# A two-layer decoder step on one core: the 796 steps of its attention stage in another order

## The chip, the core and the metric

The kernel runs on one core of a Trainium2 chip. The core has a matrix engine (TensorE, PE in the profile, its weight loads PEld), VectorE (DVE), ScalarE (ACT), GpSimd (POOL) and SyncE (SP), each with its own instruction queue that it works off in order, and 16 DMA engines that every queue's transfers share. The metric is the time of one execution in device microseconds, and lower is better.

## The reference

One inference step of a small decoder for two groups of tokens with the same weights: a prompt of 512 tokens, and 8 samples of one token each at position 2048, with a cache of 128 keys and values per sample. Two layers; each is half a SwiGLU, a mixer, half a SwiGLU. Layer 0 mixes by causal pooling, layer 1 by sliding-window attention with a sink per head. The change lies in layer 1's attention alone:

```python
kv = _rmsnorm(x, kv_norm_g) @ w_kv                       # shared keys and values, 4 heads of 64
...
h = _rmsnorm(x, norm_g[l, 1])
q = _rope((h @ w_q[j]).reshape(B, T, N_KV_HEADS, GROUP, HEAD_DIM), pos)      # 16 heads of 64
out = _window_attention(q, kk, vv, wb, pos0, attn_sinks[j]) @ w_o[j]
...
def _sink_attention(q, k, v, mask, sinks):
    s = jnp.einsum('bnqkgd,bnskd->bnkgqs', q, k) * (HEAD_DIM ** -0.5)
    s = jnp.where(mask, s, -jnp.inf)
    m = jnp.maximum(jnp.max(s, axis=-1, keepdims=True), sink)
    p = jnp.exp(s - m)
    denom = jnp.sum(p, axis=-1, keepdims=True) + jnp.exp(sink - m)
    return jnp.einsum('bnkgqs,bnskd->bnqkgd', p / denom, v)
```

D_MODEL is 1024, the window 128, everything float32.

## The kernel before, in words

Each float32 operand of a large product is split into a high part (ACT) and a low part (DVE), and a product is three passes: high by high, low by high, high by low. All 520 tokens lie along the free side of the tiles, so a matmul of the projections streams 260 columns.

The attention stage (`with tc.tile_pool(name="at" ...)`, from L1940) comes after layer 1's first half SwiGLU and before its second. Its work is cut into 796 steps. A step is a letter and a number: the letter is a function, the number which piece of it. The string `PLAN` (L61) lists them, and the loop at the end of the stage (L2349) emits them in that order. Since each emitted instruction is kept in program order (`later`), **the order of PLAN is the order in each engine's queue**, for DMAs on SP and POOL too; nothing reorders them. An engine whose first instruction waits holds up all behind it.

The steps that matter here:

- `q0` to `q63` (PE, L885): the query projection, 8 tiles t of 8 steps, 6 matmuls each. `o0` to `o63` (PE, L885): the output projection. These are the dense products.
- `e` (ACT, L1966) copies a finished query tile from PSUM to SBUF (`qraw`). For the rotary embedding the rotated rows of two or four tiles are gathered into one tile `qG` by small DMAs, 16 rows each: `a` on SP and `g` on POOL (L1974). `r` (DVE, L1980 to L1983, four instructions) rotates `qG`; `J` on SP and `I` on POOL (L1988) send the rows back. The tiles are gathered in three sets: `GATHERS = ((0, 1), (2, 3), (4, 5, 6, 7))`.
- `z`, `y` (L1992, L1995) split a tile's prompt queries. `k` (POOL, L2000) copies its sample queries to `qz`, two small copies a tile, `qz` 0 for tiles 0 to 3 and `qz` 1 for 4 to 7.
- Prompt attention goes in 16 units (a tile t, a half h of the blocks): `S` scores (PE, L2025), `N` sinks (POOL, L2034), `X` mask and minimum (DVE, L2044), `E` exponentials (ACT, L2061), `R` inverse (DVE), `C`, `c`, `p` scaling (L2072 on DVE or POOL, L2070 on ACT), `T` transposes (PE, L2083), `t`, `u` their splits (ACT L2088, DVE L2093), `V` products with the values (PE, L2110), `v`, `j` copies out (L2119).
- Sample attention: `10` to `17` scores (PE, L2158) with `b` (DVE, L2163); `20` a transpose, `B0`, `x0`, `D0` its softmax, `30` back, `d0`; `40` to `47` values (PE, L2204) with `f`. Steps `1` and `4` are matmuls that stream only 8 columns.
- `w`, `W` split weights (ACT L452, DVE L456); `l0` to `l6` (SP, L625) load the chunks of 1 MB in two DMAs (`raw`); `L0` (SP, L2283) loads the 1 MB of cached values (`vc`).
- `h`, `H`, `s`, `G` split the attention's output for `o`; `O` adds to the residual stream.

Some buffers are few: PSUM holds two double banks (query tiles, scores, output tiles) and four single ones (transposes, value products, sample products), `sm` (scores) has 3 buffers, `raw` 3, `qG` 1.

Of the kernel before, what the change touches and what calls it, by code (L numbers as in the profile page):

```python
# [58 lines left out]


PLAN = """  # L61
q0 N0 q1 q2 q3 q4 q5 q6 w6 W6 q7 e0 w10 W10 U0 q8 q9 q10 q11 q12 q13 Z0 w7 q14 q15 N1 w5 q16 g0 q17 q18 q19 a0
e1 w8 W5 q20 q24 q25 W8 q26 q27 W7 q28 q29 w15 g1 a1 r0 I0 J0 z0 y0 q21 q22 q23 e2 q30 q31 e3 S0 F0 I1 w9 S1
X0 X3 X1 X2 J1 q32 q33 q34 g3 E0 E1 S2 S3 W9 w11 w13 W13 X4 z1 y1 q35 q36 a2 X7 E2 q37 q38 E3 w12 q39 a3 g2 E4
X5 R0 e4 c1 X6 r1 W12 S4 S5 X8 q40 N2 X11 c2 c0 p3 X9 q41 W11 E6 X10 T0 T1 N3 t0 E8 q42 E5 l0 J2 w16 E7 I2 E9
W15 E10 E11 R2 C10 R1 c9 q43 q44 q45 I3 C5 c6 q46 q47 e5 C4 S6 S7 J3 l1 a4 z2 p11 X12 X15 T2 w14 t1 q48 p7 y2
X14 X13 k0 T3 t3 u1 t2 z3 q49 q50 E12 E14 W14 u0 E15 N4 E13 S8 S9 X16 W16 X18 p8 T4 X19 k3 k1 R3 C15 p13 k2
w18 t4 q51 q52 a5 L0 p12 u4 X17 E16 q53 q54 q55 E18 E17 e6 T5 S10 C14 S11 w17 q56 q57 t5 u5 q58 q59 q60 N5 u3
q61 q62 i0 q63 w19 g6 g5 X20 E20 X23 E23 X22 W17 g4 Q0 E19 R4 p18 c16 T6 T7 X21 E21 y3 a6 E22 R5 C21 C22 S12
C17 e7 u2 T8 t6 S13 g7 u6 p20 V0 W18 t8 V1 v0 V4 V5 t7 X24 a7 N6 X25 X27 u8 v1 p23 v5 v4 E24 E27 T10 r2 J4 J5  # L70
p19 w23 S14 J6 12 13 b1 t10 V2 V3 u10 v2 W19 T9 t9 S15 X26 v3 u7 I6 T11 E26 V6 t11 u9 I4 E25 J7 R6 X28 h0 N9
V8 V9 N7 X29 v9 E28 u11 z4 10 11 b0 I7 V7 X30 c25 X31 V10 y4 v6 E29 E30 I5 z5 y5 E31 V11 R7 p24 T12 t12 u12 v7
k4 h1 l2 S18 S19 v8 v10 X36 p26 p27 X37 v11 X38 S16 H1 k7 k5 k6 14 p29 T13 X39 E36 t13 16 17 b3 15 z7 p28 E38
S17 E37 b2 20 N8 p30 T14 u13 X32 V12 V13 S20 S21 p31 T15 B0 E39 R9 p37 p39 X33 x0 X35 X34 D0 30 t14 E32 u14
E35 S22 S23 y7 E33 d0 z6 p36 p38 y6 X40 X41 E34 40 42 N10 t15 u15 T18 R8 p34 p32 v13 X43 v12 E40 E43 E41 p33
T19 X44 X45 N11 43 41 f0 t19 X42 E42 u19 R10 44 45 h2 47 46 f1 s1 X47 t18 V14 S24 T16 c40 u18 t16 p35 T17 s2
c41 S25 X46 H2 H0 V18 G2 N12 X48 t17 X50 X49 p42 X51 E44 E45 V15 v14 S26 V19 s0 v15 u16 h3 H3 s3 G3 T20 G0 p43
E46 E47 G1 R11 E48 E51 S27 p44 T21 u17 p46 o0 o1 o2 E50 t20 X52 X55 c45 o3 O0 u20 V16 V17 X54 t21 p47 E49 v18
R12 v19 j16 j17 h4 l3 o4 T22 u21 p50 p48 p49 o5 s4 T23 X53 N13 o6 o7 C51 O1 t22 u22 S28 S29 T24 S30 S31 t23
X56 N14 X58 u23 w22 t24 X59 E52 E55 E53 X57 T25 E54 t25 u25 E56 R13 p53 N15 V22 V23 X60 o8 o9 o10 o11 c54 W23  # L80
u24 j23 V24 X62 X61 E57 V20 V21 X63 w21 p52 T26 W22 o24 E58 o25 c55 O2 o12 E60 E62 w28 o26 H4 E63 E59 t26 G4
v22 o27 E61 R15 R14 T27 j21 V25 p61 t27 u27 O6 p59 w26 o13 o14 o15 c63 w20 v20 h5 p58 C62 W20 v24 W26 H5 o16
o17 o18 w30 p60 T30 W21 C57 T31 t31 o19 O3 t30 C56 u31 u26 o28 o29 T28 t28 u28 T29 o30 t29 w24 u29 V26 o31 O4
V27 u30 V30 o20 o21 o22 W28 W30 v26 l4 V28 V31 v27 v25 o23 h6 H6 V29 s5 G5 W24 O7 O5 o32 o33 w25 j30 W25 s6
o36 o37 j31 w27 W27 v29 v28 h7 G6 H7 s7 G7 o34 o35 o38 O8 o39 O9 P0 Y0 o40 o41 A0 M0 A1 M1 w31 o42 W31 l5 o43
O10 P1 Y1 w35 W35 o44 o45 A2 M2 P2 Y2 o46 o47 O11 w36 W36 o48 o49 o50 o51 w29 W29 O12 P3 Y3 A3 M3 A4 M4 P4 w33
Y4 o52 o53 o54 o55 O13 W33 w32 W32 o56 P5 Y5 o57 o58 o59 O14 A5 P6 M5 o60 o61 Y6 o62 l6 o63 O15 A6 M6 w34 W34
P7 Y7 A7 M7
"""

GATHERS = ((0, 1), (2, 3), (4, 5, 6, 7))
# [2515 lines left out]
```

## Time and profile before

| what | time |
|---|---|
| runs | 1536.85, 1537.49, 1537.56 us (median 1537.49) |
| profiled execution | 1536.74 us |
| its span, first to last instruction | 1535.0 us |
| attention stage, first `q` to last `o` matmul | 1039.6 to 1197.5 us of the span |
| mean granted TensorE clock | 0.993 |

The profile's times are microseconds from the span's start. In the views by windows, each row is a stretch of the span: its length, then the busy time of each engine with the number of instructions, the granted clock of TensorE (1.00 is full speed), the mean busy share of the 16 DMA engines and GB/s. In the timeline a row is one instruction, or several alike: start, time taken, engine, line, operation, output tile <- input tiles, shapes, count, and in brackets the time for which the engine had sat idle before it and what ended that.

### The profile page before, as it was taken

The numbers are of one execution on the slowest core, as the hardware profiler recorded it, in microseconds if no ns is written. First come the engines' busy times: TensorE is split into PE (matmuls) and PEld (weight loads), VectorE is DVE, ScalarE is ACT, GpSimd is POOL, SyncE is SP. The second block draws the span as 40 slices with busy tenths as digits, with TensorE's granted clock in tenths as the row PEclk, the third lists the DMA queues.
The fourth block names the chain that finished last, engine by engine and source line by source line (L and its number), as shares of the span: only waits on it lengthen the run. The fifth ranks groups of instructions, "written<-read, shape, count | busy, mean of one in ns | idle before, by whom it ended". The sixth has DMA issues, their size and how long they took to land. (4 is left out here: it accounts for less than half of the span.)

```text
span 1535.0 us, 34974 instructions
## 1 busy us (share of the span) xinstructions
PE 1511.8 (98%) x13350; PEld 1496.5 (97%) x13350; DVE 1380.3 (90%) x2794; ACT 993.9 (65%) x2024; POOL 304.4 (20%) x346
## 2 busy tenths in 40 slices
PE   9999999999999999999999999999999999999997
PEld 9999999999999999999999999999889999999997
DVE  6999999879999999888999999886778899999976
ACT  6765765657775765656765665665776666666655
POOL 1122222001122222101322222101541122222200
PEclk9999999999999999999999999999979999999999
DMA  9589999754599999745899899763412589999941
GB/s 237 122 194 207 186 199 200 183 161 123 123 202 195 191 201 197 170 134 129 193 192 207 186 200 207 164 179 88 101 29 56 131 182 197 193 199 197 207 119 57
DMA packets 418837, 254.64 MB, mean 166 GB/s; under 512 B 13134, under 2 KB 399174, under 8 KB 418628
## 3 DMA queue, kind: packets, MB, share of 16 engines
q1 hardware_dynamic: 339390, 187.30, 44.2%
q0 software_dynamic: 75520, 60.00, 28.3%
q10 hardware_dynamic: 3758, 5.09, 1.1%
q8 instruction: 105, 1.72, 0.5%
q14 instruction: 64, 0.52, 0.1%
HBM read 218.07 MB, written 6.11 MB: 146 GB/s over the span
## 5 line engine op out<-in xcount | busy, mean ns | idle before, releaser
L452 ACT ACTIVATE wh<-raw 128x512 fp32r<-128x512 f32 (+1 forms) x724 | 445.9, 625 | 188.3 <-PE ps L915 105.9
L456 DVE TENSOR_TENSOR wl<-raw,wh 128x512 fp32r<-128x512 f32 (+1 forms) x724 | 488.1, 685 | 32.5 <-ACT wh L452 31.0
L915 PE MATMUL ps<-th,wh 128*128 128x260 f32 x1216 | 334.7, 275 | 2.5 <-DVE sb L1221 2.4
L915 PE MATMUL ps<-tl,wh 128*128 128x260 f32 x1216 | 334.4, 275 | 0.0
L915 PE MATMUL ps<-th,wl 128*128 128x260 f32 x1216 | 334.4, 275 | 0.0
L915 PE MATMUL ps<-xh,wh 128*128 128x260 f32 x896 | 246.8, 275 | 0.8 <-ACT ps L1195 0.5
L915 PE MATMUL ps<-xl,wh 128*128 128x260 f32 x896 | 246.6, 275 | 0.0
L915 PE MATMUL ps<-xh,wl 128*128 128x260 f32 x896 | 246.4, 275 | 0.0
L915 PEld LDWEIGHTS ps<-th,wh 128*128 128x128 f32 x1216 | 231.0, 190 | 3.1 <-DVE sb L1221 2.8
L915 PEld LDWEIGHTS ps<-th,wl 128*128 128x128 f32 x1216 | 231.0, 190 | 0.0
L915 PEld LDWEIGHTS ps<-tl,wh 128*128 128x128 f32 x1216 | 231.0, 190 | 0.0
L629 POOL DMA_DIRECT2D S<-in_ffn_w_up_dram x76 | 99.7, 1318 | 453.7 <-DMA S<-in_ffn_w_up_dram 145.8
L915 PE MATMUL ps<-hh,wh 128*128 128x260 f32 x656 | 181.1, 276 | 1.0 <-ACT ps L1260 0.7
L915 PE MATMUL ps<-hl,wh 128*128 128x260 f32 x656 | 181.1, 276 | 0.3 <-DVE hl L604 0.3
L915 PE MATMUL ps<-hh,wl 128*128 128x260 f32 x656 | 180.4, 275 | 0.0
L915 PEld LDWEIGHTS ps<-xh,wh 128*128 128x128 f32 x896 | 170.2, 190 | 1.4 <-ACT ps L1260 0.7
L915 PEld LDWEIGHTS ps<-xl,wh 128*128 128x128 f32 x896 | 170.2, 190 | 0.3 <-DVE xl L604 0.2
L915 PEld LDWEIGHTS ps<-xh,wl 128*128 128x128 f32 x896 | 170.2, 190 | 0.0
L352 POOL DMA_DIRECT2D raw<-raw x108 | 95.4, 883 | 337.2 <-DVE wl L456 89.0
L915 PEld LDWEIGHTS ps<-hh,wh 128*128 128x128 f32 x656 | 124.6, 190 | 2.2 <-ACT ps L1260 2.1
L915 PEld LDWEIGHTS ps<-hl,wh 128*128 128x128 f32 x656 | 124.6, 190 | 1.2 <-DVE hl L604 0.5
L915 PEld LDWEIGHTS ps<-hh,wl 128*128 128x128 f32 x656 | 124.6, 190 | 0.0
(380 smaller groups left out, 3669.0 us busy)
## 6 DMA issues: line engine op xcount, KB each, us to landing
raw<-in_ffn_w_gate_dram SPq DMA_DIRECT2D x87, 512.0 KB, 5.0
raw<-in_ffn_w_up_dram SPq DMA_DIRECT2D x87, 512.0 KB, 6.1
raw<-in_ffn_w_down_dram SPq DMA_DIRECT2D x128, 256.0 KB, 5.2
raw<-raw POOLq DMA_DIRECT2D x108, 256.0 KB, 4.5
S<-in_ffn_w_up_dram SPq DMA_DIRECT2D x76, 256.0 KB, 3.7
S<-in_ffn_w_up_dram POOLq DMA_DIRECT2D x76, 256.0 KB, 5.5
raw<-in_ffn_w_down_dram SPq DMA_DIRECT2D x16, 768.0 KB, 4.5
S<-in_ffn_w_down_dram SPq DMA_DIRECT2D x32, 256.0 KB, 4.0
```

The costliest lines, as they stand in the source:

```text
L352: G.dma_start(blk(raw, 2, 1), blk(raw, 1, 1), accum_op=ALU.add)
L452: self.pin(self.nc.scalar.activation(views[0], src, AF.Copy))
L456: self.pin(self.nc.vector.tensor_tensor(l, src, h.bitcast(F32), op=ALU.subtract))
L629: return [ld(lambda t: t, a), lambda t: nc.gpsimd.dma_start(t, b, accum_op=ALU.add)]
L915: T.matmul(bank[:, :H], a[:, kk, :], two(b), start=(not more and kk == 0 and i == 0), stop=(kk == 3 and i == 2), skip_group_check=more,)
```

## The change

`PLAN` alone is replaced. The 796 steps are the same, each once, with the same functions, engines, buffers and bytes; only their order is another. Two of the lines that are replaced, and two that replace them:

```diff
-k4 h1 l2 S18 S19 v8 v10 X36 p26 p27 X37 v11 X38 S16 H1 k7 k5 k6 14 p29 T13 X39 E36 t13 16 17 b3 15 z7 p28 E38
-S17 E37 b2 20 N8 p30 T14 u13 X32 V12 V13 S20 S21 p31 T15 B0 E39 R9 p37 p39 X33 x0 X35 X34 D0 30 t14 E32 u14
...
+R7 v10 S18 k5 z6 k6 p28 S19 X36 X39 X37 16 17 N8 E36 v9 E39 S17 X32 14 V6 X38 X33 p30 p29 b3 E38 X34 V7 X35
+p31 E37 v7 15 R9 v8 p39 p36 S20 b2 20 S22 h2 T14 p38 T15 B0 x0 t14 S23 D0 30 t15 S21 H2 d0 40 u14 v6 p37 V12
```

Three places show how it moves instructions.

**SP's queue of DMAs in the stage**, from the second set of gathers on (L1974 gathers, L1988 sends back, `raw` from `in_w_o_dram` is a weight chunk in two DMAs, `vc` the cached values). Before:

```order
L1974 DMA qG<-qraw 16x520 x2
L625 DMA raw_16128<-in_w_o_dram 64x4x512 x2
L1988 DMA qraw<-qG 16x520 x2
L625 DMA raw_16195<-in_w_o_dram 64x4x512 x2
L1974 DMA qG<-qraw 16x520 x2
L2283 DMA vc<-in_cache_v_win_dram 128x8x256
L1974 DMA qG<-qraw 16x520 x2
L1988 DMA qraw<-qG 16x520 x4
L625 DMA raw_16703<-in_w_o_dram 64x4x512 x2
```

Now:

```order
L625 DMA raw_15869<-in_w_o_dram 64x4x512 x2
L1974 DMA qG<-qraw 16x520 x2
L1988 DMA qraw<-qG 16x520 x2
L625 DMA raw_16269<-in_w_o_dram 64x4x512 x2
L2283 DMA vc<-in_cache_v_win_dram 128x8x256
L1974 DMA qG<-qraw 16x520 x4
L1988 DMA qraw<-qG 16x520 x4
L625 DMA raw_17209<-in_w_o_dram 64x4x512 x2
```

The first chunk (`l0`) now stands ahead of the second set's gathers, the second chunk and `vc` stand together ahead of all of the third set. The chunk behind the last four sends (`l2`) waited before for DVE's last split of an earlier chunk; it now takes the buffer of `vc`, and waits for the last sample value product (`46`).

**POOL's queue around the third set's sends** (L2072 is `p`, L2034 `N`, L2000 the copies to `qz`). Before:

```order
L1988 DMA qraw<-qG 16x520 x2
L2034 COPY sm<-nsinks 128x4 x2
L1988 DMA qraw<-qG 16x520 x2
L2072 TENSOR_SCALAR sm<-sm,den 128x128
L2000 COPY qz_15661<-qraw 64x8 x2
L2072 TENSOR_SCALAR sm<-sm,den 128x256 x2
L2000 COPY qz_15661<-qraw 64x8 x6
```

Now:

```order
L1988 DMA qraw<-qG 16x520 x3
L2034 COPY sm<-nsinks 128x4
L1988 DMA qraw<-qG 16x520
L2072 TENSOR_SCALAR sm<-sm,den 128x128
L2072 TENSOR_SCALAR sm<-sm,den 128x256 x2
L2034 COPY sm<-nsinks 128x4
L2000 COPY qz_15661<-qraw 64x8 x8
```

One `N` instead of two stands between the sends, and all eight copies to `qz` 1 stand together, behind three `p`.

**PE's queue at the sample values** (`40` to `47`, L2204, a row of x2 is one step). Before, with two pairs of transposes (L2083) between:

```order
L2204 MATMUL pv_16870<-prT,vc 128x8 x4
L2083 MATMUL pv_16880<-ident,sm 128x128 x4
L2083 MATMUL pv_16897<-ident,sm 128x128 x4
L2204 MATMUL pv_16870<-prT,vc 128x8 x4
L2204 MATMUL pv_16922<-prT,vc 128x8 x8
```

Now, from the first of them:

```order
L2204 MATMUL pv_16838<-prT,vc 128x8 x2
L2110 MATMUL pv_16844<-xh,tl 128x256 x2
L2110 MATMUL pv_16844<-xl,tl 128x256
L2204 MATMUL pv_16838<-prT,vc 128x8 x2
L2110 MATMUL pv_16844<-xh,tl 128x256 x2
L2110 MATMUL pv_16844<-xl,tl 128x256
```

Each step now has products with the values (L2110) or transposes beside it; six steps in a row have become at most two.

More of the change, by code (lines that the diff above doesn't have):

```diff
@@ L61 @@
 PLAN = """
[L62 to L71, printed above, removed]
@@ L72 @@
-V8 V9 N7 X29 v9 E28 u11 z4 10 11 b0 I7 V7 X30 c25 X31 V10 y4 v6 E29 E30 I5 z5 y5 E31 V11 R7 p24 T12 t12 u12 v7
-k4 h1 l2 S18 S19 v8 v10 X36 p26 p27 X37 v11 X38 S16 H1 k7 k5 k6 14 p29 T13 X39 E36 t13 16 17 b3 15 z7 p28 E38
-S17 E37 b2 20 N8 p30 T14 u13 X32 V12 V13 S20 S21 p31 T15 B0 E39 R9 p37 p39 X33 x0 X35 X34 D0 30 t14 E32 u14
-E35 S22 S23 y7 E33 d0 z6 p36 p38 y6 X40 X41 E34 40 42 N10 t15 u15 T18 R8 p34 p32 v13 X43 v12 E40 E43 E41 p33
-T19 X44 X45 N11 43 41 f0 t19 X42 E42 u19 R10 44 45 h2 47 46 f1 s1 X47 t18 V14 S24 T16 c40 u18 t16 p35 T17 s2
@@ L77 @@
[L77 to L86, printed above, removed]
@@ L87 @@
-Y4 o52 o53 o54 o55 O13 W33 w32 W32 o56 P5 Y5 o57 o58 o59 O14 A5 P6 M5 o60 o61 Y6 o62 l6 o63 O15 A6 M6 w34 W34
-P7 Y7 A7 M7
+N1 q8 N0 w5 q9 q0 q1 q2 q3 q4 q5 w13 q10 q11 q12 q6 q7 q13 q14 w6 W6 e0 g0 a0 w9 q15 e1 g1 U0 W5 q16 q17 a1 r0
+J0 I0 w10 W10 q18 q19 q20 Z0 J1 w7 W7 z0 y0 l0 I1 q21 q22 q23 e2 q24 q25 q26 q27 q28 q29 q30 q31 w8 S2 S3 F0
+e3 W8 X4 X7 X6 w15 N2 X5 q32 E4 q33 E6 W15 q34 q35 W9 E7 E5 R1 S0 S1 C5 z1 W13 X0 X2 C4 a3 X3 X1 c6 q36 q37 y1
+q38 g3 E0 E1 g2 T2 q39 E3 e4 a2 k0 S4 S5 t2 r1 w11 X8 w12 E2 R0 X9 c1 q40 q41 J2 c0 p7 c2 T3 t3 I2 q42 X11 W11
@@ new lines @@
+E8 E11 X10 E10 q43 q44 E9 I3 N3 T0 w14 u3 p3 S6 S7 W12 z2 X12 X15 X14 q45 J3 q46 q47 R2 z3 X13 y2 p8 E12 E13
+e5 E14 p11 W14 E15 R3 c9 C15 T1 t1 u2 q48 q49 q50 p12 k3 S8 T4 l1 q51 p13 C10 S9 w17 X16 C14 T5 t5 w16 L0 q52
+y3 t4 w22 q53 q54 q55 t0 N4 X18 E16 e6 a6 X19 E19 X17 E17 a4 k1 S10 g6 a5 u1 E18 S11 N5 k2 X20 X21 X23 E20 E23
+X22 g4 g5 R4 c16 Q0 C17 E22 W16 E21 W22 q56 q57 q58 q59 q60 q61 q62 p18 w18 q63 e7 u0 T6 u4 T7 t7 p19 S12 S13
+R5 V4 i0 g7 C22 t6 u5 V5 v5 10 N6 v4 u7 X24 a7 X26 p23 X25 11 E24 C21 X27 E27 E25 b0 r2 V2 V3 v3 p20 V0 v2 J4
@@ new lines @@
+u6 S14 I4 E26 T10 t10 T11 I6 I5 t11 u10 V1 v1 u11 N7 v0 S15 T8 w19 R6 T9 V10 I7 X28 X30 t8 u8 12 13 c25 V11 t9
+p24 E28 E30 X31 E31 V8 z4 J6 b1 u9 T12 t12 X29 p27 y4 V9 J5 p26 T13 t13 u13 S16 N9 v11 k4 J7 k7 z5 u12 E29 y5
+R7 v10 S18 k5 z6 k6 p28 S19 X36 X39 X37 16 17 N8 E36 v9 E39 S17 X32 14 V6 X38 X33 p30 p29 b3 E38 X34 V7 X35
+p31 E37 v7 15 R9 v8 p39 p36 S20 b2 20 S22 h2 T14 p38 T15 B0 x0 t14 S23 D0 30 t15 S21 H2 d0 40 u14 v6 p37 V12
+E32 41 E34 E33 u15 X40 X41 N10 V13 43 h0 E35 R8 p33 W17 X43 X42 E40 E41 v13 v12 V14 y6 T18 t18 E42 u18 V15 E43
@@ new lines @@
+p32 T16 S24 42 R10 v14 t16 T19 S25 p35 f0 v15 p34 u16 V16 p43 t19 h1 X44 X45 N11 E44 V18 T17 t17 u19 X46 E46
+X47 E47 44 47 h3 N12 X48 E45 c40 X51 X50 X49 V19 p42 u17 c41 v19 S26 S27 H1 v18 z7 45 46 R11 f1 s1 T20 T21 V17
+H0 s0 p47 G0 X52 s2 E48 G2 G1 H3 p44 o4 p46 t20 E50 X54 s3 G3 E51 c45 X55 X53 o5 E49 R12 o6 t21 o7 T22 u21 y7
+p50 o0 T23 t23 N13 E52 W19 C51 j16 O1 o1 E54 u20 o2 o3 E53 N14 O0 W18 E55 S28 S29 j17 o24 o25 o26 V20 o27 R13
+l2 X56 X59 X57 p49 p48 T24 X58 h4 c54 V21 S30 t22 u22 O6 E56 w23 W23 T25 t24 u24 t25 o8 o9 o10 o11 V22 j21 N15
@@ new lines @@
+p52 E57 E58 l3 u23 V23 S31 E59 R14 O2 p59 C56 w21 C57 T28 c55 u25 s4 o28 o29 o30 j23 X60 v20 w20 H4 X62 V24
+X61 v22 w24 p58 E60 X63 E63 T29 o31 W20 o16 t28 o17 t29 u29 p53 E61 E62 R15 c63 p61 W21 o18 h5 O7 H5 T26 u28
+T27 t27 u27 o19 C62 V25 w25 p60 T30 o12 T31 t30 u30 o13 o14 t26 s5 G5 o15 w31 W31 V30 t31 u31 V31 l4 O4 w29
+u26 V26 W24 V28 w26 W26 V27 v27 o20 o21 O3 o22 o23 G4 v25 o32 j30 V29 v24 v26 h6 o33 s6 W29 v29 G6 O5 W25 o36
+o37 v28 j31 h7 H6 o34 s7 H7 G7 o35 O8 w28 W28 w27 W27 o38 o39 o40 o41 o42 A0 M0 o43 P0 Y0 O9 O10 w30 W30 P1 Y1
@@ L89 @@
+A1 M1 P2 Y2 o48 o49 w32 o44 l5 l6 o45 o46 o47 o56 o57 W32 O11 w34 W34 A2 M2 o50 A3 M3 o51 O12 o52 P3 o53 Y3
+o54 o55 w36 W36 A4 M4 o58 P4 Y4 o59 O13 P5 w33 O14 Y5 o60 o61 W33 A5 M5 o62 w35 o63 O15 P6 Y6 A6 M6 A7 M7 P7
+Y7 W35
 """
```

## The prediction, made before the change was run

> **What bounds the kernel now.** I read the page first, for which engine is full. Its part on busy times, and in its slices the row of the granted clock:
>
> ```profile
> PE 1511.8 (98%) x13350; PEld 1496.5 (97%) x13350; DVE 1380.3 (90%) x2794; ACT 993.9 (65%) x2024; POOL 304.4 (20%) x346
> ...
> PEclk9999999999999999999999999999979999999999
> ```
>
> The matrix engine is full, so time can only come from its gaps, its clock or its work. The work is the same here. One slice, the 30th, has a clock of 0.7, and it lies in the attention stage. So I took the view by windows: the stage in three parts (query projection; attention proper; from the first `o` on), then short windows around the clock's edges.
>
> ```profile
> core 0: us, PE busy (x) PEld busy (x) DVE busy (x) ACT busy (x) POOL busy (x), PEclk, DMA share, GB/s
> 1039.60:1093.77 54.17, 53.37 (x492) 51.49 (x491) 37.66 (x109) 34.44 (x93) 16.06 (x35) 1.00 0.42 104
> 1093.77:1139.46 45.69, 41.95 (x317) 37.53 (x315) 33.89 (x116) 32.28 (x101) 23.39 (x40) 0.81 0.25 55
> 1139.46:1197.47 58.01, 57.95 (x521) 56.93 (x520) 47.79 (x106) 39.87 (x99) 10.82 (x16) 1.00 0.22 60
> 1113.12:1123.36 10.24, 9.56 (x50) 9.11 (x52) 8.09 (x31) 8.71 (x29) 6.99 (x9) 0.50 0.01 2
> 1130.19:1137.02 6.83, 6.83 (x35) 5.71 (x36) 5.43 (x22) 3.83 (x13) 2.33 (x3) 0.50 0.70 157
> ...
> 1126.77:1130.19 3.42, 3.42 (x33) 3.42 (x32) 3.06 (x16) 2.26 (x8) 3.11 (x5) 1.00 0.00 0
> 1109.71:1113.12 3.41, 0.58 (x12) 0.44 (x8) 0.54 (x1) 1.20 (x4) 0.74 (x4) 1.00 0.26 46
> ```
>
> All that is lost lies in the middle part: two stretches at clock 0.50, 10.24 and 6.83 us, though PE is "busy" in them. The last two rows are the 3.4 us ahead of each: before the first PE is almost idle, before the second it is busy throughout. PE's timeline says with what, and what half the clock does to a product:
>
> ```profile
> 1101.08 0.39 PE L2110 MATMUL pv<-xh,tl 128*128 128x256 f32 x2
> ...
> 1101.42 0.39 PE L2110 MATMUL pv<-xh,tl 128*128 128x256 f32 x2
> ...
> 1113.80 0.99 PE L2158 MATMUL pv<-qz,kc 128*128 128x8 f32 x4 [3.51 <-issue]
> ...
> 1120.73 0.63 PE L2110 MATMUL pv<-xh,tl 128*128 128x256 f32 x2
> ...
> 1121.37 0.63 PE L2110 MATMUL pv<-xh,tl 128*128 128x256 f32 x2
> ...
> 1127.01 2.74 PE L2204 MATMUL pv<-prT,vc 128*128 128x8 f32 x24
> ```
>
> Three value products start 0.34 us apart at full clock (1101.08 to 1101.42) and 0.64 us apart in the first stretch (1120.73 to 1121.37): half the clock costs half the stretch. It follows a wait of 3.51 us for `qz`. The second follows 24 matmuls of 8 columns in 2.74 us.
>
> **What the wait hangs on.** The timelines of SP and POOL, and the landing times of the tile `qraw`:
>
> ```profile
> 1103.76 27.28 SPq L625 DMA_DIRECT2D raw<-in_w_o_dram  x4
> ```
>
> ```profile
> 1101.53 1.03 POOL L1988 DMA_DIRECT2D qraw<-qG  x2 [2.82 <-DVE sT L2163]
> 1103.97 0.32 POOL L2034 COPY sm<-nsinks 128x4 f32<-128x4 f32 x2 [1.41 <-PE pv L2083]
> 1104.48 0.96 POOL L1988 DMA_DIRECT2D qraw<-qG  x2 [0.20 <-issue]
> 1106.29 0.42 POOL L2000 COPY qz<-qraw 64x8 f32<-64x8 f32 x2
> 1106.81 1.82 POOL L2072 TENSOR_SCALAR sm<-sm,den 128x256 f32<-128x256 f32 x2
> 1111.95 0.67 POOL L2000 COPY qz<-qraw 64x8 f32<-64x8 f32 x3 [2.06 <-DMA qraw<-qG]
> ```
>
> ```profile
> DMA to landing us min/median/max: 1.8/1.9/6.9
> ```
>
> Two of POOL's four sends stood behind an `N` that waited 1.41 us for transposes, and went out at 1104.48, behind a weight chunk of 1 MB issued at 1103.76. The last landed after 6.9 us instead of 1.9; the last copies to `qz` came at 1111.95.
>
> **The change, part by part.**
>
> *The `qz` wait, -3.51 us.* Now one `N` stands between the sends, and the chunk behind them waits for step 46, long after. The chain from the end of the query projection, by these rows:
>
> ```profile
> 1093.97 0.60 ACT L1966 COPY qraw<-ps 128x520 f32<-128x520 f32 x1
> ```
>
> ```profile
> 1098.42 0.73 DVE L1980 STREAM_SHUFFLE rp<-qG 128x520 f32<-128x520 f32 x1
> ...
> 1100.54 0.70 DVE L1983 TENSOR_TENSOR qG<-qG,rp 128x520 f32<-128x520 f32 x1
> ```
>
> Copy done 1094.6; two gathers (0.5 us to issue, 1.9 to land), 1097.3; the rotation took 2.82 us (1098.42 to 1101.24), so 1100.1; three sends, an `N`, a send (0.5, 0.2), 1102.3; three `p` (2.4: two full ones took 1.82, the third is half as wide) and an `N`, while the last send lands, 1104.9; eight copies at 0.21, 1106.6. PE gets to the first sample product of `qz` 1 (step 16) later: it worked from 1093.77 to 1110.29 before it waited, 16.5 us; of that `V6`, `V7` (12 matmuls at 0.11) go behind and `T13` (0.4) comes ahead, so 15.6 us, 1109.4. The chain is some 2.8 us early: no wait.
>
> *The first half-clock stretch, -4.78 us:* (10.24 - 0.68) / 2, since PE still waited in its first 0.68 us. What is late next: the eight steps `10` to `17` now come as 8, 8, 8, 4 and 4 matmuls with scores or value products between.
>
> *The second, -3.41 us:* 6.83 / 2. The six steps in a row of 24 matmuls become at most two (8). Before, 8 in one window left the clock up:
>
> ```profile
> 1125.19 1.06 PE L2204 MATMUL pv<-prT,vc 128*128 128x8 f32 x8
> ```
>
> *What the closed-up middle part asks of DVE, +1.7 us.* Without wait and half clock PE needs 45.69 - 3.51 - 4.78 - 3.41 = 33.99 us there, and 1.0 more for `V16` and `V17`, which now come ahead of the first `o`: 35.0. DVE was busy 33.89. The new order takes two `y`, one `W` and `G3` out of the middle part (0.6 each, 0.1), and trades `C17` and `u2` for `u4` and `u5`: net 1.8 less, so 32.1 of 35.0, 92%. DVE works off its queue in order and stalls too; its share in slices of the stage in which PE hardly waited:
>
> ```profile
> 1070.00:1080.00 10.00, 9.20 (x86) 8.40 (x85) 8.74 (x28) 7.78 (x25) 4.09 (x6) 1.00 0.37 82
> 1080.00:1090.00 10.00, 10.00 (x97) 9.44 (x97) 7.87 (x26) 8.93 (x26) 6.96 (x18) 1.00 0.61 165
> 1090.00:1100.00 10.00, 9.78 (x89) 8.76 (x87) 9.19 (x30) 7.09 (x22) 4.93 (x7) 1.00 0.06 15
> ```
>
> At 0.919 it needs 34.9 us and costs nothing; at 0.787, where PE was the bound, 40.8, 5.8 more than PE. I take 0.874, where each waited for the other in turn: 36.7, so 1.7 us of small waits, the likeliest at the sample softmax (20, `B0`, `x0`, `D0`, 30) and ahead of the first `o`, which needs `H0` and `G0`. Both ends count for the range.
>
> *At nothing:* the query steps in another order, `q8` and `q9` first (the same 64 steps at full rate; cover is PE's own work). The first chunk behind `J1` on SP: the sends it can slow are those of tile 1, wanted at `S4`, some 8 us later; uncovered 5 us. The second chunk and `vc` ahead of the third set's gathers: three of the four tiles' can be slowed, but all wait for the last tile's. The last five weight loads come no later, and `W35`, now last, is the fourth tile of the next stage. Other small waits (0.5, 0.3, 0.2 us in the first two parts) I take to come again in like number.
>
> *Sum:* 3.51 + 4.78 + 3.41 - 1.7 = 10.0 us off. The profiled execution took 1536.74 us (span 1535.0 and 1.74 around it), so 1526.7; the median of the runs stands 0.75 above it: **1527.5**. Without any new wait 1525.8.
>
> **The rivals.**
>
> *A half-clock stretch comes back.* Steps 16, 17, 14 and 15 put 16 short matmuls into some 3.5 us, more than the 8 in a window that did no harm, fewer than the 24 that did. For it: all that stands near are scores, transposes and two value products, and in the second stretch 3.4 us of such did not bring the clock back. Against: value products stand between. Two windows at half clock cost 3.4 us, 1530.9; three 5.1, 1532.6. [...]
>
> *DVE stalls as in 1080 to 1090* (0.787): 5.8 in place of 1.7, 1531.6. For it: long chains by ACT. Against: most units have some 10 us between `S` and `T`.
>
> *The sends are slow after all,* so that the change doesn't do what it says. 6.9 for 1.9 us brings the copies to 1111.6, PE waits 2.2 us and the first stretch at half clock returns: 2.2 + 4.8, 1534.5. Against: no load is due near 1100.
>
> *Slower: the clock falls at step 16 and stays down till the first `o`.* From there on PE has 1139.46 - 1113.80 - 4.78 - 3.41 = 17.5 us, and the moved value products 2.3: 19.8. At half clock that is 19.8 more, less the 1.7 that it hides: 1545.6. It decides if no window of the mixed order is busy enough to raise the clock. Against: windows that were mostly value products raised it at 1123.36 and 1137.02.
>
> **How the numbers follow.** Forecast 0.61, half clock once more 0.24, DVE 0.05, slow sends 0.06, slower 0.04. The range takes in the first three, from below the sum without new waits to above three windows: 1524.0 to 1533.0. A measurement of this kernel can tell about 0.2%, 3.1 us, from no change: under 1534.4 is faster. That is the first three and some of the sends, 0.91; same 0.05; slower 0.04.
>
> **What would show it.** In the changed profile: no wait over 1 us at L2158; landing of `qraw` at most some 2.5 us; clock 1.00 in every window of the stage; the middle part 36 to 38 us long, with DVE at 0.85 or more. Wrong would make it: a clock of 0.50 anywhere in the stage, or waits of PE for DVE or ACT adding up to over 4 us.

## The result, and the profile after

| | before | after |
|---|---|---|
| runs, median | 1536.99 us (6 runs, 1534.79 to 1537.56) | 1526.89 us (6 runs, 1526.02 to 1532.45) |
| profiled execution, span | 1536.74, 1535.0 us | 1526.27, 1524.5 us |
| mean granted clock | 0.993 | 0.998 |

The ratio of the two is 0.9943, with a 95% interval of 0.9927 to 0.9958. In the profiled executions the difference is 10.47 us. The page of the changed kernel, its busy times and its slices of the clock:

```profile
PE 1503.9 (99%) x13350; PEld 1489.7 (98%) x13350; DVE 1378.9 (90%) x2794; ACT 992.4 (65%) x2024; POOL 307.7 (20%) x346
...
PEclk9999999999999999999999999999999999999999
```

The 0.7 in the 30th slice is gone. PE is busy for 7.9 us less with the same 13350 matmuls; the "busy" time that went was matmuls at half clock (9.56 and 6.83 us in the two stretches, half of which is 8.2). The view by windows of the changed kernel, the stage in the same three parts (query projection; attention proper; from the first `o` on; columns as in the prediction):

```profile
1039.15:1093.08 53.93, 53.43 (x490) 51.42 (x489) 38.18 (x113) 33.93 (x92) 18.44 (x36) 1.00 0.43 104
1093.08:1129.63 36.55, 35.61 (x325) 31.90 (x324) 31.38 (x110) 32.78 (x103) 23.98 (x41) 1.00 0.05 11
1129.63:1187.10 57.47, 57.19 (x512) 56.14 (x511) 48.44 (x109) 38.42 (x95) 12.32 (x15) 1.00 0.44 102
```

54.17, 45.69 and 58.01 us became 53.93, 36.55 and 57.47: 9.92 of the 10.47 us come from the stage, 9.14 of them from its middle part, where the clock is now 1.00 throughout. All that is left of waits of PE in that part (engine, line, releaser: us in total, times, longest):

```profile
PE pv L2158 <- POOL qz L2000: 0.3, 1, 0.3
PE pv L2176 <- DVE sT L2163: 0.3, 1, 0.3
PE pv L2193 <- ACT xh L2088: 0.2, 1, 0.2
```

The wait of 3.51 us is 0.33. Not all of it had been for `qz`: before, the last copy ended at 1112.63 and PE started at 1113.80, and the profile names nothing that it waited for in these 1.17 us. The gap is 1.18 us in `b_load` below; it went together with the wait, and its cause is open. POOL's timeline of the changed kernel shows the chain to `qz`, and the last line, of the landings of the sends in 1095 to 1110, that none landed late (before, up to 6.9):

```profile
1100.87 1.50 POOL L1988 DMA_DIRECT2D qraw<-qG  x3 [4.20 <-DVE qG L1983]
1102.37 0.21 POOL L2034 COPY sm<-nsinks 128x4 f32<-128x4 f32 x1
1102.50 0.49 POOL L1988 DMA_DIRECT2D qraw<-qG  x1
1103.02 2.40 POOL L2072 TENSOR_SCALAR sm<-sm,den 128x128 f32<-128x128 f32 x3
...
1105.51 2.40 POOL L2000 COPY qz<-qraw 64x8 f32<-64x8 f32 x8
```

```profile
DMA to landing us min/median/max: 1.9/2.0/2.1
```

### The profile page after: what moved, and what is told of

It reads as the page before. It is cut to its first block, busy times and chain, and to the rows that moved or that the text cites. A ratio compares the mean times of both kernels' runs of the same rounds, so it can differ in the third digit from the quotient of the medians.

```text
span 1524.5 us, 34971 instructions
## 1 busy us (share of the span) xinstructions
PE 1503.9 (99%) x13350; PEld 1489.7 (98%) x13350; DVE 1378.9 (90%) x2794; ACT 992.4 (65%) x2024; POOL 307.7 (20%) x346
## 4 chain that ended last, share of the span: by engine, by line
PE 84%; DVE 9%; ACT 3%; issue 2%; DMA 1%; POOL 0%; ACTq 0%; DVEq 0%
PE ps L915 62%; PE ps L885 17%; DVE wl L456 2%; ACT wh L452 1%; PE pv L2110 1%; DMA pr<-in_bands_dram 1%; PE ps L2025 1%; PE pv L2083 1%; DVE tl L604 0%; DVE x L1720 0%; PE ps L2477 0%; DVE raw L366 0%; PE pv L885 0%; DVE wl L427 0%; PE ps L1538 0%
```

## The experiments

Two theories stood at the start. **A**, the prediction's: the gain is the wait for `qz` and the two stretches at half clock; a window of 3.41 us that starts anywhere and holds too little full-rate work for PE halves the clock for the next. The 3.41 us are read from the trace of before: its clock changes at 1113.12, 1123.36, 1130.19, 1137.02 and 1529.55 us, and the stretches between, 10.24, 6.83, 6.83 and 392.53 us, are 3, 2, 2 and 115 times 3.413. **B**, in several forms: other parts of the new order carry it, or only an idle PE lowers the clock. Edits of PLAN are shown as fragments of its lines; "before" and "changed" say which order was edited. A window at half clock is put at 3.41 / 2 = 1.7 us of PE, an estimate from the value products of before, three of which start 0.64 us apart in it and 0.34 at full clock.

### The changed kernel again, twice

> The changed kernel once more, for a second trace and more times; nothing is edited. Of its first six times five lay at 1526.0 to 1528.3 us and one at 1532.45, with a mean clock of 0.993 in place of 0.998. Theory A: windows of 3.41 us that run free of the program, in another phase in every execution, decide the clock; the thinnest 3.4 us of the stage (about 1107.4 to 1110.8, where steps 16, 17 and 14 put 12 short matmuls beside a wait for qz) drop it where they fill one window. Then most times lie at 1526 to 1528.5, about one in six at 1530 to 1533 and few between; the phase of the clock's edges in this trace against its first instruction differs from that in the first trace (2.65 us modulo 3.413). Rival B: the time of 1532.45 was a disturbance from outside. Then no time over 1529 comes again, or one with the clock at 0.998. If the phase is fixed to the program's start, the edges stand at 2.65 modulo 3.413 again.

Measured: 1527.58 us (5 runs, 1525.67 to 1528.18), 0.9938 of before, 0.9925 to 0.9950. The time of over 1529 did not come again here. The view by windows of this trace:

```profile
69.35:72.76 3.41, 1.49 (x14) 1.30 (x12) 3.41 (x7) 2.22 (x6) 0.49 (x1) 1.00 1.01 215
72.76:76.18 3.42, 3.42 (x18) 3.42 (x17) 3.37 (x7) 0.97 (x2) 0.79 (x1) 0.50 1.27 301
```

A window in which PE was busy for 1.49 of 3.41 us is followed by one at half clock, 1000 us ahead of the attention stage. It was not in the first trace of this kernel, with the same instructions. What differs is the phase: the edges of the clock's stretches, modulo 3.413 us from the first instruction, are one number for each execution and another in the next (2.65 us in the first trace of this kernel, 1.08 in this one). Over all 14 traces of this study, worked out from their clock records:

```
remainder of the edges (us)              half-clock window near 73 us
0.03 0.37 0.38 1.97 2.24 2.65 2.84
2.95 3.36 3.37                           no  (10 executions)
1.08 1.10 1.20 1.74                      yes (4 executions)
```

So the windows run free of the program, and which of its thin places fills one is drawn anew with each execution. The changed kernel a third time, beside later runs:

> The changed kernel a third time, as the measure for the three kernels beside it on the same chip. Expected 1526 to 1528.5, some of its executions 1.7 us longer by one window at half clock near 73 us (long before the attention stage), as in the second one's trace, and perhaps one above 1529 (a window at half clock in the stage, from about 1107 on). The middle part, from the last copy e7 to the first o matmul, 36.4 to 36.7 us.

Measured: 1526.77 us (1526.15 to 1529.15), 0.9940 of before (0.9927 to 0.9952); the middle part is 36.3 us long from `e7`'s copy to the first `o`. Of the 16 times of the changed kernel two are over 1529: 1529.15 (clock 0.996) and 1532.45 (0.993).

### The sends: behind the load, or late?

The first try moved `l2` in the order before:

```diff
-k4 h1 l2 S18
+k4 h1 S18
...
-47 46 f1 s1
+47 46 l2 f1 s1
```

> The order before, with one step moved: the weight load l2 stands behind step 46 in place of behind h1, so no large load is under way when the last two sends of qraw go out at about 1104.5; the two N steps still stand ahead of those sends. Theory A (the 1 MB load ahead of them made the sends land after 6.9 us): the sends land after at most 2.5 us, qz is done by about 1110, PE waits at most 0.5 us at L2158, the stretch at clock 0.50 from 1113 on is gone, the second one (after 24 short matmuls in a row) stays: -3.5 - 4.8, so 1536.7 - 8.3 = about 1528.5. Rival B (their late issue behind the N steps is enough): they land at about 1106.5 all the same, but PE still waits 1 to 2 us for qz and the clock still falls: 1533 to 1536.

Measured: 1536.39 us, ratio 1.0000 (0.9991 to 1.0009). The edit changed nothing on the chip, as SP's timeline shows:

```profile
1100.72 2.41 SPq L1988 DMA_DIRECT2D qraw<-qG  x4
1103.19 1.34 SPq L625 DMA_DIRECT2D raw<-in_w_o_dram  x2
```

The load went out right behind the sends, since SP's queue held nothing between the old place and the new, and a later place in PLAN is no wait. This run tells nothing of either theory, except what such an order is worth. Two further edits did what was meant, one on either side:

```diff
-E25 J7 R6 X28 h0 N9 V8 V9 N7 X29 v9 E28 u11 z4 10 11 b0 I7
+E25 J7 I7 I5 R6 X28 h0 N9 V8 V9 N7 X29 v9 E28 u11 z4 10 11 b0
```

(`I5` leaves its place further on.)

> The order before, with two steps moved: the sends I7 and I5 stand ahead of N9 and N7, so all four of POOL's sends go out by about 1102.6, ahead of the 1 MB load l2, which stays where it was (issued at 1103.76). Theory A (the load delays what goes out after it): all sends land after at most 2.5 us, the wait of 3.5 us at L2158 and the first stretch at 0.50 are gone, the second stays: about 1528.5. Rival B (l2 slows what is still under way, or the copies to qz wait for something else): landings over 3 us and a wait over 1 us stay, and the time is 1531 or more.

Measured: 1531.21 us (1530.07 to 1533.24), 0.9966 (0.9953 to 0.9978).

```diff
-v2 W19 T9
+v2 T9
...
-k4 h1 l2 S18
+k4 h1 S18
...
-47 46 f1 s1
+47 46 W19 l2 f1 s1
```

> The order before, with W19 and then l2 moved behind step 46, so that l2 takes the buffer of vc and its transfers wait for the last sample value product: now no large load is under way when I7 and I5 go out, late, at about 1104.5 (the two N steps still stand ahead of them). This is what b_load was meant to be; there the load still went out at 1103.19, since a place further on in PLAN made it wait for nothing new. Theory A (a send lands late only behind a large load): all sends land after at most 2.2 us, the last copies to qz are done at about 1110, when PE gets there: a wait of at most 0.5 us, no first stretch at 0.50, the second one stays; about 1528.5 to 1530.5 (b_sinks, with the sends ahead of the load, came to 1531.2). Rival B (the N steps ahead of the sends cost the time): a wait of 1 us or more at L2158, clock falls, 1533 to 1537.

Measured: 1531.54 us (1530.08 to 1533.94), 0.9971 (0.9960 to 0.9981). The landings of the last sends in `b_sinks`, and then in `b_late`:

```profile
DMA to landing us min/median/max: 1.9/2.0/2.0
```

```profile
DMA to landing us min/median/max: 1.7/1.9/1.9
```

In `b_late` they went out as late as before, with no load ahead of them, and landed in 1.9 us: it was the load that made 6.9 us of it, and going out late cost no more than 0.6 us of waiting. PE's waits for `qz` fell to 0.6 us in both (each profile has the first of these lines; the second is of `b_sinks`):

```profile
PE pv L2158 <- POOL qz L2000: 0.6, 1, 0.6
PE pv L2193 <- ACT sm L2061: 1.0, 1, 1.0
```

Both times miss what was expected: `b_sinks` by 2.7 us (1528.5), `b_late` by 1.0 (at most 1530.5). In `b_sinks` 0.6 us of the wait for `qz` is left, and PE now waits 1.0 us at step 30, a wait that the order before did not show; the rest is not traced. The second stretch stayed in both, as expected. But `b_late` shows what the wait had hidden (view by windows):

```profile
1110.43:1113.84 3.41, 2.83 (x28) 2.53 (x28) 3.39 (x14) 3.27 (x10) 3.26 (x6) 1.00 0.00 0
1113.84:1117.26 3.42, 3.42 (x19) 3.20 (x20) 2.68 (x12) 3.42 (x13) 2.08 (x3) 0.50 0.02 5
```

Without the wait, the 16 short matmuls of steps 14, 16, 17 and 15 in one window, with 0.6 us of waiting, still drop the clock, for one window in place of three. That is 1.7 us of `b_late`'s profiled execution. In `b_sinks`, at another phase, no window there was thin enough. The first stretch was thus two causes in one place: the wait, which made it three windows, and the old run of sample scores.

### Short matmuls in a row, with no wait

```diff
-V13 43 h0 E35
+V13 h0 E35
...
-p32 T16 S24 42 R10
+p32 T16 S24 43 42 44 47 45 46 R10
```

(`f1` follows `f0`; 44, 47, 45 and 46 leave their later places.)

> The changed order, but with 43, 42, 44, 47, 45 and 46 in a row at the place of 42: 24 short matmuls in some 2.7 us, as before the change, with no wait ahead of them. Theory A (a window with too little streamed through PE halves the clock, idle gap or not): a stretch at 0.50 of two or three windows (6.8 or 10.2 us) follows wherever the row fills most of a window, +3.4 to +5.1 us, so 1530 to 1532; where a window's edge cuts the row in the middle the clock stays and the time is that of the changed kernel, near 1527; so the times fall into two groups, the higher one the larger. Rival (only an idle gap of PE lets the clock fall): clock 1.00 in all the stage and a median within 1 us of the changed kernel's 1526.9.

Measured: 1530.71 us (1529.22 to 1531.87), 0.9962 (0.9950 to 0.9975): 3.1 us above the same kernel without the row (1527.58, run beside it). Four of the times lie at 1530.7 to 1531.9, one at 1529.22, with a clock of 0.998. PE's timeline, the windows, and a wait that the row brought:

```profile
1120.35 0.27 PE L2025 MATMUL ps<-tl,xh 64*128 64x128 f32 x2
1120.55 3.62 PE L2204 MATMUL pv<-prT,vc 128*128 128x8 f32 x24
```

```profile
1119.00:1122.41 3.41, 3.41 (x34) 3.17 (x32) 2.31 (x9) 2.68 (x9) 3.41 (x4) 1.00 0.00 0
1122.41:1129.24 6.83, 6.83 (x34) 6.27 (x35) 3.45 (x14) 1.68 (x5) 0.36 (x2) 0.50 0.54 115
```

```profile
PE pv L2083 <- ACT sm L2070: 1.3, 1, 1.3
```

By the profile PE was busy for 3.41 of 3.41 us, and the clock fell: it takes no idle gap, and the rival falls. Before the change the second stretch began in the same way, behind a window in which PE was busy for 3.42 of 3.42 us.

The 3.1 us are not the clock's alone. In the trace the stretch costs 3.4 us, and the row also brings the wait of 1.3; the one time with the clock at 0.998 still lies 2.1 us or more above those of the changed kernel with that clock (1525.67 to 1527.06).

### What a window must hold

The 14 traces have 663 windows at full clock in and around the stage. For each I added up the matmuls that start in it, at their spacing at full clock from the timelines (0.112 us for a projection or value product, 0.11 for a transpose, 0.077 for a score, which runs in pairs on 64 rows, 0 for one of 8 columns), as a share of 3.413 us. Twelve windows were followed by half clock; the table has them, and four of the thinnest that kept it:

```
share  short  window from  kernel    next        share  short  window from  kernel    next
0.17   16     1110.4       b_late    0.50        0.40   17     1119.0       a_row     0.50
0.18    0     1109.7       before    0.50        0.42    8     1124.2       b_both    0.50
0.23   24     1126.8       before    0.50        0.44    0     1108.2       b_load    0.50
0.26   24     1125.2       b_load    0.50        0.47   13     1128.1       a_dve     1.00
0.26   23     1120.7       b_late    0.50        0.50    8     1109.3       a_best    0.50
0.35   19     1118.1       b_sinks   0.50        0.50    0     1129.2       a_row     1.00
0.39   16     1110.5       b_both    0.50        0.50   12     1120.8       b_both    1.00
0.40   12     1109.7       a_relief  0.50        0.53   12     1115.4       after     1.00
```

All eleven at 0.44 or less lost the clock, and all but one of the 652 at 0.47 or more kept it. In these traces the limit lies near 0.45 to 0.5 of a window, whether idle time or short matmuls thin it. The measure is mine, and its weights were chosen with these windows in view: with the transposes at 0 the two kinds overlap (0.47 lost the clock, 0.23 kept it). No run varied the share alone.

### Is it the middle part alone?

```diff
-E25 J7 R6 X28 h0 N9
+E25 J7 I7 I5 R6 X28 h0 N9
...
-E34 40 42 N10 t15 u15 T18 R8 p34 p32
+E34 40 N10 t15 u15 T18 R8 p34 42 p32
...
-N11 43 41 f0 t19 X42 E42 u19 R10 44 45 h2 47 46 f1 s1
+N11 V14 43 41 f0 V15 44 t19 X42 E42 u19 R10 S24 45 h2 v14
```

(47 follows T17, 46 follows V18, with `f1`, `s1`, `s2` behind it.)

> The order before, with two local edits together: the sends I7 and I5 ahead of N9 and N7 (as in b_sinks), and the eight sample value steps 40 to 47 spread between value products, transposes and scores, with their neighbours (S24, V14, V15 come earlier, f1, s1, s2 later). All else of the 796 steps keeps its old place. Theory A (the gain of the whole change is the wait, the two stretches at half clock and nothing else): no 0.50 in the stage in most executions, and 1526.5 to 1528.5, as the changed kernel (1527.6 and 1526.9). Rival C (the rest of the new order carries a part of the gain: query steps, weight splits, the loads): 1529 to 1531 with the clock at 1.00 all through the stage.

Measured: 1533.62 us (1531.20 to 1535.82), 0.9984 (0.9975 to 0.9993): a miss. The windows say why:

```profile
1110.54:1113.95 3.41, 3.40 (x30) 3.08 (x31) 3.25 (x12) 3.33 (x9) 3.41 (x5) 1.00 0.00 0
1113.95:1117.36 3.41, 3.41 (x21) 3.19 (x21) 2.73 (x15) 3.41 (x15) 2.07 (x3) 0.50 0.02 5
1124.19:1127.60 3.41, 2.50 (x26) 2.17 (x26) 2.69 (x9) 3.10 (x9) 0.64 (x2) 1.00 0.00 0
1127.60:1134.43 6.83, 6.83 (x38) 5.79 (x35) 4.41 (x22) 3.73 (x16) 2.33 (x3) 0.50 0.38 93
```

The sample scores stayed in their old run (16 short in the first of these windows), and my spread of the value steps made a new idle place: in 1124.19 to 1127.60 PE was busy for only 2.50 us. Taking the matmuls apart by hand moved the thin place rather than closing it. A cleaner cut answers the question: the old order up to `e7`, then the steps that are left, in the new order (no diff is shown: it is the new PLAN behind `e7`).

> A mixture: the order before for all steps up to e7 (the whole query projection and what stood between), then the steps that are left in the changed order. Theory A (the gain comes from the middle part alone: the wait for qz and the two stretches at half clock): 1526 to 1528.5, within 0.7 us of the changed kernel beside it. Rival C (the new order of the query steps, weight splits and first loads carries part of it): at least 1.5 us slower than the changed kernel.

Measured: 1527.52 us (1526.16 to 1529.20), 0.9942 (0.9930 to 0.9954), 0.75 above the changed kernel beside it (1526.77), a little more than the 0.7 allowed, with intervals that overlap almost wholly; its profiled execution took 1526.16 us, the changed kernel's beside it 1526.15, both with the clock at 1.00 in all the stage:

```profile
1092.90:1129.61 36.71, 35.59 (x324) 31.72 (x322) 32.47 (x113) 32.64 (x102) 24.39 (x42) 1.00 0.05 11
```

So the old query steps, splits and early loads give away nothing that these runs can tell: what gains is the order from `e7` on.

### DVE in the closed-up part

Seven copies moved onto DVE:

```diff
-R7 v10 S18
+R7 j10 S18
...
-N8 E36 v9 E39
+N8 E36 j9 E39
```

(and 8, 6, 13, 12, 15 likewise.)

> The changed order, with seven copies of the value products (6, 8, 9, 10, 12, 13, 15) on DVE (j) in place of ACT (v), all in the middle part: 7 x 0.43 = 3.0 us more for DVE, 7 x 0.37 = 2.6 less for ACT. DVE was busy 31.28 of 36.45 us there. Theory A of the prediction (DVE is what the closed-up middle part works against, at a share of 0.87 of the time): 34.3 / 0.874 = 39.2, so +2.8 us, 1530.3, or at least +0.8 if DVE can reach 0.92. Rival B (the 1.5 us of small waits there are single dependences and DVE has slack of some 5 us): within 0.5 us of the changed kernel, with DVE at 0.94 of the middle part.

Measured: 1529.87 us (1528.46 to 1532.95), 0.9964 (0.9950 to 0.9977). The middle part, cut at `e7`'s copy as in `b_mid`; below it the changed kernel's by the same cut; then PE's longest wait in `a_dve`:

```profile
1095.05:1133.43 38.38, 36.15 (x323) 31.96 (x322) 33.43 (x117) 30.51 (x96) 24.28 (x41) 1.00 0.04 10
1093.28:1129.63 36.35, 35.41 (x323) 31.70 (x322) 31.18 (x110) 32.78 (x103) 23.98 (x41) 1.00 0.05 11
```

```profile
PE pv L2176 <- DVE sT L2163: 1.2, 1, 1.2
```

It is 2.03 us longer, with the clock at 1.00; DVE is busy for 2.25 us more, at 33.43 / 38.38 = 0.871 of the time (0.858 in the changed kernel). So these copies find no slack of 5 us: they cost the part nearly what they add to DVE, and 1.2 us of it shows as a wait for step 20, the sample softmax. But DVE's share alone is not the bound. In `b_mid` above DVE is busy for 32.47 of 36.71 us, a share of 0.885, 1.29 us more than in the changed kernel, and the part is only 0.36 us longer; the changed kernel itself took 36.74 in `a_again`'s trace. The likelier reading, which no run tests alone, is that it counts what stands in DVE's queue ahead of a chain that PE waits for. The other way:

```diff
-g7 C22 t6
+g7 p22 t6
...
-R8 p33 W17 X43
+R8 p33 X43
...
-X55 X53 o5
+X55 X53 W17 o1
```

(`o0` to `o3` change places with `o4` to `o7`, and `O0` with `O1`.)

> The changed order with less for DVE in the middle part: W17 (0.66 us) behind X53, with the output tiles 0 and 1 changing places so that nothing waits for it, and C22 on POOL (p22, 0.92 us there) in place of DVE (0.35): 1.0 us less of DVE's 31.3. Theory A (the middle part's remaining 1.5 us of waits come from a DVE that is nearly full, as a_dve's +3.0 us of DVE work, which made the part 1.85 us longer, says from the other side): the middle part falls from 36.4-36.7 to 35.6-36.0 and the median by about 0.6 us against the changed kernel beside it. Rival (the waits left are single chains: qz, the sample softmax): the middle part stays at 36.3 or more.

Measured: 1526.99 us (1526.35 to 1531.54), against 1526.77 of the changed kernel beside it: no gain. Its profiled execution, at 1531.54, is the slowest, and shows where such a time comes from:

```profile
1095.66:1134.73 39.07, 38.47 (x324) 34.34 (x322) 30.90 (x108) 33.06 (x103) 24.34 (x42) 0.91 0.04 10
1109.71:1113.12 3.41, 3.08 (x32) 2.73 (x31) 3.32 (x11) 3.32 (x10) 2.03 (x7) 1.00 0.02 5
1113.12:1119.94 6.82, 6.82 (x37) 5.90 (x37) 4.26 (x19) 4.40 (x15) 6.00 (x7) 0.50 0.00 0
```

That is the place of steps 16, 17 and 14, unedited here: with a window that starts at the wait for `qz`, its 12 short matmuls and 0.33 us of waiting (a share of 0.40) drop the clock for two windows. It is the prediction's first rival, caught once. Without it the part would be 39.07 - 3.41 = 35.7 us long, in theory A's span, but 1531.54 less its three windows at half clock (these two and one near 350 us, 1.7 each) is 1526.4, no shorter than the 1526.15 and 1526.27 of the changed kernel's executions that had none; whether less for DVE helps stays open.

### Two tries at a better order

```diff
-X39 X37 16 17 N8 E36 v9 E39 S17 X32 14 V6 X38
+X39 X37 V6 16 S17 17 V7 N8 E36 v9 E39 X32 14 15 X38
...
-S20 b2 20 S22 h2
+S20 b2 S22 20 h2
```

(`V7` and `15` leave their later places.)

> The changed order, with its thinnest place evened out: V6 ahead of 16, S17 and then V7 between and behind 16 and 17, 15 beside 14, S22 ahead of 20. Theory A (a window whose share of full-rate products is under about 0.45 halves the clock; of the changed kernel the place from 1107.4 on has a share of 0.36 in the worst phase): the worst share over all phases rises to about 0.45 to 0.5 and no time lies over 1529; the qz wait (0.3) goes and the one at 20 (0.3) with it, so the median falls by 0.3 to 0.8 against the changed kernel on the same chip (1527.6). Rival B (the place does not matter, the variation among times comes from elsewhere in the kernel, as the half-clock window at 72.76 in the trace of the changed kernel's second run): the times spread from 1525.5 to 1528.5 as before and the median is the same.

Measured: 1527.64 us (1525.96 to 1532.39), 0.9949 (0.9935 to 0.9962). No gain: the waits at 16 and 20 went, and one came at step 30 in their place. Nor did the times over 1529 go, as theory A had it: 1532.39 came at a clock of 0.996, in an execution without a trace, so what made it is not known.

```profile
1115.15 0.30 PE L2193 MATMUL pv<-ident,pr 128*128 128x128 f32 x1 [0.95 <-DVE pr L2189]
```

Then `a_relief` with one more edit:

```diff
-X39 X37 16 17 N8 E36 v9 E39 S17 X32 14 V6 X38
+X39 X37 V6 16 17 N8 E36 v9 E39 S17 X32 14 X38
```

> As a_relief, and with V6 ahead of 16. Theory A: the wait of 0.3 us for qz goes too, and the thinnest place of the changed order (steps 16, 17 and 14 beside that wait, a share of full-rate products of 0.36 in the worst phase, where all windows at 0.44 or less were followed by half clock and all at 0.47 or more were not) rises to 0.47 or more at that place, so that no window there can halve the clock: the middle part is 35.3 to 35.7 us, the median 0.8 to 1.0 us below the changed kernel beside it, and no time lies over 1529. Rival: the waits come again elsewhere (at 20 and 30), and nothing is gained.

Measured: 1528.91 us (1527.67 to 1533.21), 2.1 above the changed kernel beside it. Nothing is gained, as the rival said, though not by new waits alone: with `V6`'s value products gone from behind 14, a window at that place lost the clock. Theory A had called it safe at a share of 0.47 or more; it had 0.50, the one exception above.

```profile
1109.28:1112.69 3.41, 2.94 (x29) 2.62 (x28) 3.30 (x17) 3.23 (x12) 3.41 (x5) 1.00 0.02 5
1112.69:1116.10 3.41, 3.41 (x17) 2.63 (x19) 1.72 (x6) 2.26 (x7) 3.41 (x5) 0.50 0.00 0
```

No version beat the changed kernel.

## Why the prediction was right

1526.89 us stand against 1527.5 foretold, inside the range. Three of the four signs that it named are in the profile: no wait over 1 us at L2158, the clock at 1.00 in the whole stage, and a middle part of 36 to 38 us with DVE above 0.85. The fourth, landings of `qraw` within 2.5 us, holds for the sends (2.1); the gathers, which the same view counts in, took up to 3.5. By its steps:

- **The `qz` wait, foretold -3.51, measured -3.18.** The mechanism held from both sides: just behind a load of 1 MB the last send landed after 6.9 us (7.0 in `b_load`), ahead of the load after 2.0 at most (`b_sinks`), with none under way after 1.9 (`b_late`). The slack was mis-sized: 2.8 us foretold, -0.3 measured. The last gathers took 3.4 us to land, not the 1.9 of the other small transfers (2.1 for the same two before), though no load was under way. The trace's DMA packets show what was: one of 16 KB on the queue that the page calls q8, instruction, ran from 1095.07 to 1096.18. Of the 16 packets of each gather 15 had started by 1095.59, and the last started at 1096.16 and 1096.39. In all nine traces with the new order behind `e7` such a packet holds up a last gather like this, in the five with the old order it comes after them and they land in 1.9 to 2.2 us. The rotation thus began at 1097.74, and the eight copies to `qz` took 0.30 us each, not 0.21. The chain ended at 1107.9; shifted to where the changed kernel's query projection ends, 0.7 us earlier than before, it was foretold for 1105.9. PE was at step 16 at 1107.63, where 1108.7 was foretold in the same way. That none of this cost more than 0.33 us was some luck.
- **The first stretch at half clock, foretold -4.78, gone.** What would be "late next", the run of sample scores, was named rightly, and `b_late`'s trace shows that without the spreading one window of the three could stay.
- **The second, foretold -3.41, gone.** `a_row` brings it back at its size (6.83 us at 0.50) by putting 24 short matmuls in a row.
- **DVE, foretold +1.7.** The part was to be 36.7 us long, 1.7 over the 35.0 that PE needs, and was 36.55, with DVE busy 0.859 of it, where I took 0.874. The length is right, the reason only in part, and that is luck. Of small waits for DVE and ACT only 0.5 us are there, at steps 20 and 30; ahead of the first `o` PE did not wait. Without any wait PE needed 36.55 - 0.83 = 35.7 us, 0.7 more than reckoned, a price that the prediction left out, most likely that of the spreading itself. A first pair of value products behind another kind of matmul stands 0.31 us from the next one, a later pair 0.22:

```profile
1109.96 0.47 PE L2110 MATMUL pv<-xh,tl 128*128 128x256 f32 x2
1110.27 0.28 PE L2110 MATMUL pv<-xl,tl 128*128 128x256 f32 x1
1110.38 0.39 PE L2110 MATMUL pv<-xh,tl 128*128 128x256 f32 x2
1110.60 0.28 PE L2110 MATMUL pv<-xl,tl 128*128 128x256 f32 x1
```

In this part PE changes from one kind to another 41 times before and 50 times now; nine changes at 0.09 us would be 0.8. That is an estimate from these rows, and no run varied it alone. `a_dve` shows that work put ahead of the sample softmax on DVE costs time there, `b_mid` that DVE's share alone does not set the length.

- **At nothing:** in the last part 0.54 us went where 1.0 was to (`V16` and `V17` moved out of it), 0.24 in the query projection, and 0.55 outside the stage, within what one execution differs from the next. By `b_mid` the query steps and early loads cost and gain nothing that these runs can tell.
- **The rivals.** A half-clock stretch coming back was given 0.24. Its two and three windows are the 6.83 and 10.24 us that half clock lasted in the trace of before; a single one, of 3.41 or 3.42 us, is in those of `b_late`, `b_both` and `a_best`. It is real at the place named, caught in `a_relief`'s trace, and drawn by phase: of the changed kernel's 16 times one (1532.45, clock 0.993) fits it, at the time that was worked out for three windows (1532.6). That this one time was that is argued from its clock; it has no trace. The other rivals did not occur.

## What to carry to other kernels

Read the clock's row before the busy rows: matmuls of 8 columns counted as busy (3.41 of 3.41 us in `a_row`) and the clock still fell to 0.50, so spread them between full ones until any 3.4 us, wherever it starts, holds well over half its time in full-rate products (here 11 of 11 windows at 0.44 or less lost the clock, and one at 0.50), and expect to pay for the spreading (here an estimated 0.09 us for a change of kind). Keep large loads from being issued just ahead of small transfers that something waits for (6.9 us to land in place of 1.9), and look in the queue, not in the source's order, whether an edit moved them: `b_load` moved a load by three lines of the list and by nothing on the chip. When gaps close, ask what stands in an engine's queue ahead of a chain that PE waits for; DVE's share alone did not tell (0.871 in `a_dve` with 2.0 us lost, 0.885 in `b_mid` with 0.4). Further hand-made swaps moved waits about rather than removed them.

## What the runs showed of the hardware

- The clock's windows run free of the program, at another phase in each execution: in 14 traces every edge of a trace shares one remainder modulo 3.413 us, and the remainders go from 0.03 to 3.37. Their length is that of the stretches (10.24, 6.83 and 392.53 us in `before` are 3, 2 and 115 of them). One program has thus several times: of the changed kernel's 16, those with a mean clock of 0.998 lie at 1525.67 to 1527.06 us, those at 0.996 and 0.997 at 1526.77 to 1529.15.
- A window with a share of full-rate work of 0.44 or less was followed by half clock in 11 of 11 cases, one with 0.47 or more in 1 of 652, whether idle time (0.18 in `before`, no short matmul) or 8-column matmuls (0.40 in `a_row`, 17 of them) thinned it.
- For the way up the limit is less sharp. Of the 23 windows at half clock in the stage, the nine with a share of 0.43 or less were followed by another at half clock; of the fourteen at 0.44 to 0.52 (value products stand 0.213 us apart there, so some 0.52 is the most) twelve were followed by full clock and two, at 0.46 and 0.50, were not.
- The last sends, of 32.5 KB each, landed in 1.7 to 2.1 us (`after`, `b_sinks`, `b_late`); the two that went out just behind a load of 1 MB landed in 4.9 and 6.9 us in `before` (4.9 and 7.0 in `b_load`). Gathers of the same size took 3.4 to 3.9 us where a 16 KB packet of the instruction queue, of 0.9 to 1.6 us, met them, and 1.9 to 2.2 where it came later.
